# Rolling a matrix by 100 columns: how the last row groups of the long copy are cut

## The chip, the cores and the metric

The kernel runs on one core of a Trainium2 chip. The metric is the device time of a run in microseconds; for the kernel before it is the median of three runs, 816.32 us (815.55 to 818.43). Beside the runs there is one profiled execution, with its own span and trace; all durations of instructions and transfers come from it.

## The reference

```python
def setup_inputs():
    return {"x": np.random.randn(8192, 8192).astype(np.float32), "shift": 100}

def reference(x, shift):
    return np.roll(x, shift, axis=1)
```

Every row of the output is the row of the input turned to the right by 100 elements: `out[r, 100:]` is `x[r, :8092]`, and `out[r, :100]` is `x[r, 8092:]`. Nothing is computed; 268.4 MB are read and 268.4 MB are written.

## The kernel before, in words

With `s = 100`, the output's columns are split at `a = 256` (the next multiple of 128 above `s`, and 128 more). The two sides take different ways.

**The long side, columns 256 to 8191** (7,936 floats, 31,744 bytes a row), is copied straight from HBM to HBM, without a tile in between, by DMAs issued from SP (`nc.sync`) and ACT (`nc.scalar`). The rows are viewed as 128 blocks `c` of 64 rows; a block holds four groups `j`, and group `j` takes the rows `64c + 4e + j` for `e` from 0 to 15, so a group has 16 rows, four apart. The views `xm` and `om` (L36 to L37 of the code below) say this. The loop runs over blocks and groups in order (L41 to L43); even groups go to SP, odd ones to ACT, so each engine has its own queue with 256 of the 512 groups. A group is one DMA of 16 rows, 496 KB; in the last four blocks, which are 16 groups, it is two DMAs of 16 half rows (3,968 floats each, split at `mid = 4224`), 248 KB each. That makes 248 whole and 16 half pieces on each queue.

The order on each queue is the program's order. The framework gives the long side's DMAs eight semaphores, four to SP and four to ACT, taken in turn (108, 111, 113, 115 on SP and 107, 110, 112, 114 on ACT); an issue waits until the DMA that used its semaphore before has landed. A DMA raises its semaphore once for each of 16 DMA engines, each of which moves one of the 16 rows. SP waits at the end for all semaphores before the program closes.

**The short side, columns 0 to 255**, is done by GpSimd (POOL) and VectorE (DVE). For each of 16 strips of 512 rows, GpSimd loads the head of the rows in three DMAs (L72, L73, L76) into SBUF tiles, VectorE copies parts of one tile into another (L74, L77), and at the end GpSimd stores 16 tiles of 512 KB (L80). It uses a queue of its own. In the profiled execution its last store lands at 505.9 us.

The few lines that decide the pieces:

```python
mid = (a + n_cols) // 256 * 128
for c in range(blocks):
    parts = ((a, mid), (mid, n_cols)) if c >= blocks - 4 and a < mid else ((a, n_cols),)
    for j in range(4):
        for lo, hi in parts:
            engines[j % 2].dma_start(out=om[c, j, :, lo:hi], in_=xm[c, j, :, lo - s:hi - s])
```

Of the kernel before, what the change touches and what calls it, by code (L numbers as in the profile page):

```python
# [1 line left out]

# [4 lines left out]


@with_exitstack
def kernel(  # L10
    ctx: ExitStack,
    tc: tile.TileContext,
    x: bass.AP,
    shift: int,
    out: bass.AP,
):
    nc = tc.nc
    n_rows, n_cols = x.shape
    s = shift % n_cols
    a = -(-s // 128) * 128  # L20
    if 0 < a <= 384 and a + 128 <= n_cols:
        a += 128
    g = a - s
    P = nc.NUM_PARTITIONS
    engines = [nc.sync, nc.scalar]
    n_chunks = 16
    rows = n_rows // n_chunks

    xm = x.rearrange("(c e j) w -> c j e w", e=16, j=4)
    om = out.rearrange("(c e j) w -> c j e w", e=16, j=4)
    if a < n_cols:  # L36
        blocks = n_rows // 64  # L37
        mid = (a + n_cols) // 256 * 128
        for c in range(blocks):
            parts = ((a, mid), (mid, n_cols)) if c >= blocks - 4 and a < mid else ((a, n_cols),)  # L40
            for j in range(4):  # L41
                for lo, hi in parts:
                    engines[j % 2].dma_start(out=om[c, j, :, lo:hi], in_=xm[c, j, :, lo - s:hi - s])  # L43
    if a == 0:
        return


    if a > 512:
        for i in range(n_chunks):
            r = slice(i * rows, (i + 1) * rows)  # L50
            nc.gpsimd.dma_start(out=out[r, :s], in_=x[r, n_cols - s:])
            if g > 0:
                nc.gpsimd.dma_start(out=out[r, s:a], in_=x[r, :g])
        return

    Q = 4  # L60
    n_st = n_rows // (P * Q)
    reads = ctx.enter_context(tc.tile_pool(name="reads", bufs=n_st))
    heads = ctx.enter_context(tc.tile_pool(name="heads", bufs=n_st))
    xt = x.rearrange("(k p q) c -> k p q c", q=Q, p=P)
    ot = out.rearrange("(k p q) c -> k p q c", q=Q, p=P)
    tiles = []
    for k in range(n_st):
        t = reads.tile([P, Q - 1, a], x.dtype)
        h = heads.tile([P, Q, a], x.dtype)
        lead = bass.AP(tensor=x.tensor, offset=(k * P * Q + 1) * n_cols - s,  # L70
                       ap=[[Q * n_cols, P], [n_cols, Q - 1], [1, a]])
        nc.gpsimd.dma_start(out=t[:], in_=lead, single_packet=True)  # L72
        nc.gpsimd.dma_start(out=h[:, Q - 1, :s], in_=xt[k, :, Q - 1, n_cols - s:], single_packet=True)  # L73
        nc.vector.tensor_copy(h[:, :Q - 1, :s], t[:, :, :s])  # L74
        if g > 0:
            nc.gpsimd.dma_start(out=h[:, 0, s:], in_=xt[k, :, 0, :g], single_packet=True)  # L76
            nc.vector.tensor_copy(h[:, 1:, s:], t[:, :, s:])  # L77
        tiles.append(h)
    for k, h in enumerate(tiles):
        nc.gpsimd.dma_start(out=ot[k, :, :, :a], in_=h[:], single_packet=True)  # L80


# [1 line left out]
_INS = ['x', 'shift']  # L84
_OUTS = [((8192, 8192), 'float32')]

_NUMBERS = {'shift': 100}


# [26 lines left out]
```

## Time and profile before

| what | value |
|---|---|
| runs, median (lowest to highest) | 816.32 us (815.55 to 818.43) |
| profiled execution, span from first to last instruction | 813.9 us |
| last landing of the long side in it | 812.95 us |
| DMA packets and bytes of the span | 22,277 packets, 276.9 MB |
| mean rate of the DMA engines | 340 GB/s |
| SP's and ACT's issues of whole pieces | 248 each, 12.5 us from issue to landing (median) |
| SP's and ACT's issues of half pieces | 16 each, 5.9 us from issue to landing (median) |
| VectorE busy | 12.0 us |
| GpSimd busy | 41.1 us |

The median of the runs stands 2.4 us above the span of the profiled execution; the page has no time for what lies around the span. The bytes are counted once for each packet, though the long side reads and writes HBM. A "GB/s" of a stretch counts the packets that start in it. A "landing" is the event at which a DMA engine raises the semaphore of the DMA; a DMA of the long side has 16 of them, and "from issue to landing" is up to the last.

### The profile page before, as it was taken

What the parts mean: (1) busy time and instruction counts of PE and PEld (TensorE: products, weight loads), DVE (VectorE), ACT (ScalarE), POOL (GpSimd) and SP (SyncE); (2) the same over time, 40 slices, a digit from 0 to 9 for tenths busy, and PEclk for the clock granted to TensorE, in tenths of its full rate; (3) what the DMA queues carried; (4) which work ended last, traced back from release to release, by engine and by line L of the source; (5) the groups of instructions that cost most, each with busy time, mean ns of one, the idle gap of its engine ahead of it and who ended that gap; (6) DMA issues with size and microseconds to landing.
All of it is one profiled execution on the core that took longest, in us unless ns stands there. A gap on an engine that the chain in (4) does not pass through costs nothing. (4 is left out here: it accounts for less than half of the span.)

```text
span 813.9 us, 689 instructions
## 1 busy us (share of the span) xinstructions
DVE 12.0 (1%) x32; POOL 41.1 (5%) x68
## 2 busy tenths in 40 slices
DVE  0000000000000000000000000000000000000000
POOL 2000011111000100000000000000000000000000
DMA  9999999999999999999999999999999999999998
GB/s 314 346 340 344 353 346 350 344 351 344 346 355 346 345 362 354 353 357 354 355 355 349 342 335 331 335 332 325 335 328 332 334 337 334 332 337 332 334 314 293
DMA packets 22277, 276.90 MB, mean 340 GB/s; under 512 B 9472, under 2 KB 9728, under 8 KB 13824
## 3 DMA queue, kind: packets, MB, share of 16 engines
q1 hardware_dynamic: 8448, 130.04, 45.9%
q10 hardware_dynamic: 8448, 130.04, 44.3%
q0 software_dynamic: 5376, 16.78, 8.9%
q14 instruction: 5, 0.04, 0.0%
HBM read 268.44 MB, written 268.44 MB: 660 GB/s over the span
## 5 line engine op out<-in xcount | busy, mean ns | idle before, releaser
L80 POOL DMA_DIRECT2D out_dram<-h x16 | 11.4, 713 | 139.5 <-DMA out_dram<-h 92.5
L76 POOL DMA_DIRECT2D h<-in_x_dram x16 | 8.6, 540 | 158.4 <-DMA t<-in_x_dram 158.4
L72 POOL DMA_DIRECT2D t<-in_x_dram x16 | 12.2, 760 | 32.1 <-DMA h<-in_x_dram 31.3
L73 POOL DMA_DIRECT2D h<-in_x_dram x16 | 8.9, 558 | 32.7 <-DMA h<-in_x_dram 32.7
L74 DVE COPY h<-t 128x300 f32<-128x300 f32 x16 | 5.9, 367 | 268.4 <-DMA t<-in_x_dram 268.4
L77 DVE COPY h<-t 128x468 f32<-128x468 f32 x16 | 7.5, 468 | 0.0
L97 POOL MEMSET const-float32-0.0<- 128x1 f32 x1 | 0.1, 98 | 0.2 <-issue 0.2
L97 POOL MEMSET const-bfloat16-1.0<- 128x1 bf16 x1 | 0.1, 101 | 0.0
L97 POOL MEMSET const-float32-1.0<- 128x1 f32 x1 | 0.1, 98 | 0.0
L97 POOL MEMSET const-uint8-127<- 128x1 uint8 x1 | 0.1, 98 | 0.0
## 6 DMA issues: line engine op xcount, KB each, us to landing
out_dram<-in_x_dram ACTq DMA_DIRECT2D x248, 496.0 KB, 12.5
out_dram<-in_x_dram SPq DMA_DIRECT2D x248, 496.0 KB, 12.5
out_dram<-h POOLq DMA_DIRECT2D x16, 512.0 KB, 102.9
t<-in_x_dram POOLq DMA_DIRECT2D x16, 384.0 KB, 48.9
out_dram<-in_x_dram SPq DMA_DIRECT2D x16, 248.0 KB, 5.9
out_dram<-in_x_dram ACTq DMA_DIRECT2D x16, 248.0 KB, 5.9
h<-in_x_dram POOLq DMA_DIRECT2D x16, 78.0 KB, 41.9
h<-in_x_dram POOLq DMA_DIRECT2D x16, 50.0 KB, 47.2
```

What stands on the lines that cost most here:

```text
L72: nc.gpsimd.dma_start(out=t[:], in_=lead, single_packet=True)
L73: nc.gpsimd.dma_start(out=h[:, Q - 1, :s], in_=xt[k, :, Q - 1, n_cols - s:], single_packet=True)
L74: nc.vector.tensor_copy(h[:, :Q - 1, :s], t[:, :, :s])
L76: nc.gpsimd.dma_start(out=h[:, 0, s:], in_=xt[k, :, 0, :g], single_packet=True)
L77: nc.vector.tensor_copy(h[:, 1:, s:], t[:, :, s:])
L80: nc.gpsimd.dma_start(out=ot[k, :, :, :a], in_=h[:], single_packet=True)
L97: nc = _bacc.Bacc("TRN2", target_bir_lowering=False, num_devices=1)
```

## The change

Only the loop that issues the long side changes. The number of pieces of a group now depends on `left`, the number of groups from this one to the last: quarters for the last four groups, halves for the six before them, whole for all others.

```diff
         blocks = n_rows // 64
-        mid = (a + n_cols) // 256 * 128
+        def cuts(parts):
+            w = (n_cols - a) // parts // 128 * 128
+            return [(a + i * w, a + (i + 1) * w if i + 1 < parts else n_cols) for i in range(parts)]
+
         for c in range(blocks):
-            parts = ((a, mid), (mid, n_cols)) if c >= blocks - 4 and a < mid else ((a, n_cols),)
             for j in range(4):
-                for lo, hi in parts:
+                left = 4 * (blocks - c) - j
+                for lo, hi in cuts(4 if left <= 4 else 2 if left <= 10 else 1) if n_cols - a >= 512 else [(a, n_cols)]:
                     engines[j % 2].dma_start(out=om[c, j, :, lo:hi], in_=xm[c, j, :, lo - s:hi - s])
```

Halves are cut where they were (3,968 floats each). A quarter is 1,920 floats (7,680 bytes a row), the last of four 2,176 (8,704 bytes a row). Each queue then issues 251 whole pieces, 6 halves and 8 quarters, 265 in all, where it issued 248 and 16, 264 in all. The last block is all quarters, the block before it all halves, and of the block before that groups 2 and 3 are halves.

## The prediction

> **What bounds the kernel now.** I read the page first: its engine rows, its row of DMA shares and its queues. No engine computes on the path (VectorE 1% of the span, GpSimd 5%), the 16 DMA engines are at nine tenths or more in 39 of 40 slices, and the two hardware queues, SP's and ACT's, carry 260 of 277 MB:
>
> ```profile
> q1 hardware_dynamic: 8448, 130.04, 45.9%
> q10 hardware_dynamic: 8448, 130.04, 44.3%
> q0 software_dynamic: 5376, 16.78, 8.9%
> ```
>
> The columns are packets, MB and the share of the 16 engines' span. 8448 packets for 264 DMAs of a queue are 32 each: 16 of data, one row for each engine, and 16 that raise the semaphore. The third queue, GpSimd's column strip, has its last landing at 505.9 us (semaphore events of the trace), so nothing of it is left in the stretch that the change touches. The page's chain of waits ends on GpSimd and does not follow SP to the end; I don't use it. The view of the waits, for SP's queue, does:
>
> ```profile
> SPq L43 <- DMA out_dram<-in_x_dram: 667.0, 260, 4.5
> SPq L111 <- DMA out_dram<-in_x_dram: 5.4, 4, 2.4
> ```
>
> Of its 264 issues 260 wait for an earlier transfer, 667.0 us in all: only the first four don't. The issues' semaphores say which: each queue has four, taken in turn, so issue i waits until issue i-4 of its queue has landed on all 16 engines. **Eight pieces are in flight, whatever their size**: 8 x 508 KB of wholes, 8 x 254 KB of halves (a piece is 16 rows of 31,744 or 15,872 bytes). The second line is the drain behind SP's last issue. The source view of the copy line, over 700 to 781 us (wholes) and over 781 to 814 us (halves), gives the time from issue to landing:
>
> ```profile
> L43 SPq DMA_DIRECT2D out_dram<-in_x_dram x27: 509/509/510, 700.0 to 778.6; - x27
> ...
> DMA to landing us min/median/max: 11.2/12.2/12.8
> ```
> ```profile
> L43 SPq DMA_DIRECT2D out_dram<-in_x_dram x16: 509/510/510, 781.6 to 806.7; - x16
> ...
> DMA to landing us min/median/max: 4.7/5.9/9.4
> ```
>
> 12.2 us for 8 x 508 KB is 333 GB/s, 5.9 us for 8 x 254 KB is 344 GB/s: at either size what is in flight is just worked off in one round trip. Now the stretches, with DMA share and GB/s last:
>
> ```profile
> 700.00:781.00 81.00, 0.00 (x0) 0.00 (x0) 1.00 0.99 334
> 781.00:796.00 15.00, 0.00 (x0) 0.00 (x0) 1.00 0.88 301
> 796.00:811.00 15.00, 0.00 (x0) 0.00 (x0) 1.00 0.98 343
> 811.00:812.50 1.50, 0.00 (x0) 0.00 (x0) 1.00 0.11 42
> ```
>
> Wholes run at 334 GB/s; the step to halves at 781.6 us dips to 301; halves once settled are as fast as wholes. A row counts a packet where it starts, so data under way at a border must be put back: half of 16 x 31.7 KB = 0.25 MB at 781, half of 16 x 15.9 KB = 0.13 MB at 796. The step: 15 x 301 KB + 0.25 - 0.13 = 4.64 MB, 13.9 us' worth at 334 in 15.0 us, **1.1 us lost**. From 796 to the last packet's end (812.4 us): 15 x 343 + 1.5 x 42 KB + 0.13 MB = 5.34 MB, 16.0 us' worth in 16.4, **0.4 us lost**. All that a better end could win is about 1.5 us of 816, or 0.2%.
>
> **The change part by part.** The whole-row pieces grow from 248 to 251 on each queue, the halves fall from 16 to 6, and 8 quarters come last (6 of 7,680 bytes a row, 2 of 8,704). Bytes, rows, order of rows, GpSimd's work and the start are the same, so all is equal until the first half, which now goes out six groups later: 6 x 508 KB at 334 GB/s = 9.1 us after 781.6, at about 790.7 us. The data left from there are 16 - 6 = 10 groups in place of 16.
>
> (1) One more issue on each queue, 265 for 264. An issue takes 0.51 us and SP's median wait is longer; at 334 GB/s two queues need a quarter of 127 KB (the mean) every 2 x 127 / 334 = 0.76 us each, more than 0.51. Cost 0; if four issues become ready together they follow each other at 0.51 us, which 0.76 mostly covers. Upper bound one issue, 0.5 us.
>
> (2) The step from wholes to halves is moved, not removed: the same eight wholes are in flight before it. It costs the 1.1 us again. The cause is read from the landings: the first of a whole's 16 landings comes 6 us before its last (median spread 6.0 us in 700 to 781), so the fast engines have half of a 12.2 us window left, and when refills halve they run dry. In before the share stays low until 795, in after the first quarter goes out after six halves of a queue, where before had reached 792.2 us, so part of this dip runs into the next step. Change 0; bounds -0.4 (the last third left out) and 0.
>
> (3) A second step, from halves to quarters, is new. The trace has no such step; the nearest row is the first step, 1.1 us, at twice the sizes: spread of landings 2.1 us for halves (median) against 6.0, window 5.9 against 12.2. In proportion to the size it costs half: **+0.5 us**, bounds 0 (the smaller spread is covered) and +1.1 (as the first).
>
> (4) The quarters themselves. Eight hold 1.02 MB, 3.0 us of work at 334 GB/s. Their round trip has no row either. Its parts: 1.4 us from the first issue (0.74 us) to the first packet (2.14 us), 0.5 us from the last packet's end (812.43) to the last landing (812.95), and two packets' times, its own and the other queue's: a half's packet is 0.72 us in the mean (least 0.59), so 2 x 0.36. That is 2.6 us on an engine with nothing queued. On top comes the lag of the slowest engine, 2.1 us for halves; in proportion 1.0. Sum 3.6 to 4.7 us against 3.0 us of data in flight: the queue is starved. The same sum for halves, 1.9 + 1.4 + 2.1 = 5.4 us, is under their 6.1 us of data and close to the 5.9 seen, which is why halves kept the rate. Sixteen quarters are two rounds of eight; the first still has halves in front of it and is (3). The second loses 3.6 - 3.0 = **+0.6 us**; bounds 0 and 4.7 - 3.0 = +1.7. I take the lag in proportion, because it went 6.0 to 2.1 from wholes to halves.
>
> The Trainium skill, "DMA: Bandwidth & Descriptors", section on the anatomy of one DMA, fits a software-queue DMA as about 2.0 us fixed plus its bytes at 436 GB/s. By that a quarter is an estimated 2.3 us, below 3.0, nothing is starved and term (4) is 0. The rows above speak against it: the quickest half in this trace took 4.7 us, where the page's fit would give 2.6.
>
> (5) The end. When the last piece is taken up, engines finish unevenly by about one packet. The 0.4 us lost after 796 shrinks with the piece: **-0.4 us** if all goes, 0 if it was not of the end at all.
>
> Sum: 0 + 0 + 0.5 + 0.6 - 0.4 = +0.7 us. The profiled execution's span is 813.9 us, its last landing at 812.95; the runs' median, 816.32, lies 2.4 us above that span, and I carry this over unchanged: 814.6 us of span, **817.0 us** for the median.
>
> **The rivals.** A measurement of this kernel can tell about 0.3% (2.4 us) from no change; the three runs shown span 2.9 us.
>
> *No starvation.* Terms (3) and (4) at 0, the end better by 0.4, the dip cut short by 0.4: 816.32 - 0.8 = 815.5 us. For it: halves ran at 343 GB/s, so a smaller piece costs nothing by itself. Against it: the round trip's 1.9 us of fixed parts do not shrink. Within 0.3% too.
>
> *A shorter end that shows.* Every loss after 781 comes back, 1.5 us: 814.8 us. That still is only 0.2%; to be over 0.3% faster the runs must fall low as well, which the spread of the runs allows (the lowest of before is 0.8 under its median). Chance 0.15.
>
> *Starved quarters, the other sign.* In-order waits on four semaphores a queue make one slow engine hold up all eight slots; if a quarter's lag stays at the halves' 2.1 us or grows (single half packets took up to 2.0 us), both rounds are starved. The price is two rounds of (round trip - 3.0) less 0.4; it is over 2.4 us from a round trip of 4.4 us on. With 4.7 us: 2 x 1.7 - 0.4 = +3.0, 819.3 us. For it: packets' stalls come singly and need not shrink with the size. Against it: the last round drains, and the spread fell by more than half when the size halved. Chance 0.23.
>
> *The change does not do what it says.* The order of the issues on the two queues shows 251 wholes, 6 halves and 8 quarters on each, and the splits start at multiples of 512 bytes in the output; nothing to wait for is added but the four semaphores. No chance of its own.
>
> **How the numbers follow.** Within 0.3% (forecast and no starvation together) 0.62, faster 0.15, slower 0.23. The range goes from 1.5 us won with 0.4 for the runs' own scatter (814.4) to the starved case (819.3).
>
> **What would show it.** In the changed profile: stretches equal to before up to about 790; a dip to about 0.85 share behind the first half at 790.7; issue to landing of the quarters at 3.6 us, not 3.0 (covered) or 4.7 (starved); a GB/s of 260 to 290 in the last 6 us of data; the last landing at 813 to 814.5 us. I am wrong if the changed kernel's stretch before 780 us differs, since nothing there is changed, or if the settled halves no longer keep the rate of wholes.

## The result, and the profile after

| | runs | median (lowest to highest), us |
|---|---|---|
| before | 10 | 817.09 (815.45 to 818.43) |
| after | 10 | 819.44 (817.19 to 820.91) |

The ratio on record is 1.0023, with a 95% interval from 1.0013 to 1.0032: 1.9 us slower (1.1 to 2.6). The two medians of the table stand 2.35 us apart; the ratio is what is used below. On the scale of the forecast's 816.32 us that is 818.2 us, where 817.0 was forecast. The sign came out, and by the bound of 0.3% it is no change that one measurement could tell; ten runs a side can, and the forecast of +0.7 us lies below their interval.

(In the kernel before, the views stand at L34 and L35 and the loop at L39 to L43, not at L36 to L37 and L41 to L43 as said above. The copy line is L43 there and L46 in the changed kernel.)

The profiled execution has a span of 818.3 us (its run: 820.1 us). The runs from here on list a time about 1.8 us above their span; by that, before's profiled execution, with its 813.9 us, took about 815.7 us, 1.4 us under the median of ten. The page's queue rows (packets, MB, share):

```profile
q1 hardware_dynamic: 8480, 130.04, 46.3%
q10 hardware_dynamic: 8480, 130.04, 44.1%
q0 software_dynamic: 5376, 16.78, 8.2%
```

32 packets more on each queue are the one DMA more; the bytes are equal. SP's waits:

```profile
SPq L46 <- DMA out_dram<-in_x_dram: 673.0, 260, 5.3
SPq L114 <- DMA out_dram<-in_x_dram: 3.2, 1, 3.2
```

The drain behind SP's last issue fell from 5.4 to 3.2 us, as eight quarters in place of eight halves are left then. Read alone, that looks like a gain. The stretches (DMA share and GB/s last) show that it was paid for before:

```profile
700.00:781.00 81.00, 0.00 (x0) 0.00 (x0) 1.00 1.00 333
...
794.00:805.00 11.00, 0.00 (x0) 0.00 (x0) 1.00 0.87 292
805.00:815.00 10.00, 0.00 (x0) 0.00 (x0) 1.00 0.82 281
815.00:816.60 1.60, 0.00 (x0) 0.00 (x0) 1.00 0.52 167
```

The first half goes out at 794.0 us, the first quarter at 805.2. After the step to halves (0.87, as before's 0.88) the engines never fill up again: the quarters follow at a share of 0.82, where before had run at 0.98 and 343 GB/s from 796 to 811. The source view of the copy line from 805.1 us on holds the quarters alone:

```profile
L46 SPq DMA_DIRECT2D out_dram<-in_x_dram x8: 509/510/527, 805.2 to 813.3; - x8
...
DMA to landing us min/median/max: 3.0/3.8/5.1
```

3.8 us for 1.02 MB in flight is 267 GB/s.

The two profiled executions differ by 4.4 us, but not all of that is the change's. I worked out, from the packets' starts, durations and sizes, how long each execution took from the moment that N MB were left (packets under way counted in part) to its last packet's end, and took off N MB at 334 GB/s. That "loss" is compared below, since it leaves out the first 750 us, in which both kernels do the same and single executions scatter: with 20 MB left the changed kernel's execution was already 2.6 us late (753.7 us against 751.0).

| us lost against 334 GB/s in the last | 20 MB | 10 MB | 3 MB | 0.5 MB |
|---|---|---|---|---|
| before | 1.5 | 1.6 | 0.8 | 1.0 |
| after | 3.1 | 3.0 | 2.0 | 0.9 |

1.6 us of the tail are lost more, 1.2 of them in the last 3 MB, where the quarters are. These are single executions: a second one of the changed kernel (e5_after) lost 2.7 us in the last 20 MB, not 3.1.

### The profile page after: what moved, and what is told of

The parts are those of the page before. It is cut to its first block, busy times and chain, and to the rows that moved or that the text cites. A ratio compares the mean times of both kernels' runs of the same rounds, so it can differ in the third digit from the quotient of the medians.

```text
span 818.3 us, 691 instructions
## 1 busy us (share of the span) xinstructions
DVE 12.0 (1%) x32; POOL 41.3 (5%) x68
## 4 chain that ended last, share of the span: by engine, by line
DMA 32%; another core or an unknown queue 16%; POOL 1%; issue 1%; POOLq 0%; PEldq 0%
DMA h<-in_x_dram 28%; DMA t<-in_x_dram 4%; POOL out_dram L83 1%; POOL h L76 0%; POOL t L75 0%; POOLq L114 0%; POOL h L79 0%; POOLq L83 0%; PEldq L114 0%
```

## The experiments

My theory is **starvation**: eight DMAs are in flight whatever their size; the round trip, from a DMA's issue to its last landing, has parts that do not shrink with the piece; eight quarters hold less work than a round trip lasts. The rivals: the **step** (any change of size costs once), the **packet** (short packets cost by themselves), and the **stretch** (the halves' stretch was cut from 16 groups to 6, so that the step lies nearer to the end). All kernels are the changed one with another rule for the pieces; only the loop is touched.

**Sixty-four groups in quarters (e1_q64): starvation made large.**

```diff
-                for lo, hi in cuts(4 if left <= 4 else 2 if left <= 10 else 1) if n_cols - a >= 512 else [(a, n_cols)]:
+                for lo, hi in cuts(4 if left <= 64 else 1) if n_cols - a >= 512 else [(a, n_cols)]:
```

> Quarters for the last 64 groups (256 quarters), no halves. Starvation theory (eight quarters in flight, 1.02 MB, against a round trip of 3.6 to 4.0 us as in the changed kernel's profile): 32.5 MB move at 254 to 282 GB/s in place of 334, so 115 to 128 us for 97 us, 18 to 31 us slower than before, and the stretch shows that rate throughout. Step theory (only the change of size costs, once): about 2 us slower, as the change itself. Packet theory (each shorter packet costs a little by itself; an undisturbed 7,680-byte packet takes 291 ns, half of 592 is 296): no more than 2 us slower.

Measured 847.21 us, ratio 1.0356 (1.0340 to 1.0372): 29 us slower. Here are the stretch and the source view of the copy line in the middle of the quarters:

```profile
740.00:830.00 90.00, 0.00 (x0) 0.00 (x0) 1.00 0.80 255
```
```profile
L46 SPq DMA_DIRECT2D out_dram<-in_x_dram x91: 509/510/716, 739.5 to 829.8; - x91
...
DMA to landing us min/median/max: 3.1/4.0/4.6
```

One DMA in flight after another takes 4.0 us, eight of 127 KB give 8 x 127 / 4.0 = 254 GB/s, and 255 is what is seen over 90 us. That these two agree is bookkeeping: with eight always in flight they must, as they do for wholes. What says that the engines wait for work is the share of 0.80 where wholes have 0.99: a fifth of their time is idle, so neither the shorter packets nor the 16 semaphore packets of each DMA fill it. Nor is it the issuing: 91 issues of 0.51 us take 46 of SP's 90 us. 32.5 MB at 255 in place of 334 GB/s is 30 us more, and 29 were timed. The step theory (2 us) and the packet theory (2 us) fall.

**The same packets with more in flight (e2_m64).** One DMA carries the quarter of all four groups of a block, 64 rows; all groups ahead of these go whole. The lines that make the views `xb` and `ob` are left out here.

```diff
+            if c >= blocks - 16:
+                for i, (lo, hi) in enumerate(cuts(4)):
+                    engines[i % 2].dma_start(out=ob[c, :, :, lo:hi], in_=xb[c, :, :, lo - s:hi - s])
+                continue
```

> The same packets of 7,680 and 8,704 bytes for the last 64 groups, but one DMA takes a quarter of the columns of all four groups of a block: 64 rows, 4 packets for each engine, 508 KB in flight for each DMA, eight in flight. Starvation theory: as fast as whole pieces in that stretch, 334 GB/s and 12 us from issue to landing, within 1.5 us of before. Packet theory: the same loss as with 256 separate quarters. Step theory: no step in what is in flight, so as whole pieces.

Measured 819.95 us, ratio 1.0027 (1.0016 to 1.0038).

```profile
740.00:800.00 60.00, 0.00 (x0) 0.00 (x0) 1.00 0.99 329
```
```profile
L47 SPq DMA_DIRECT2D out_dram<-in_x_dram x20: 511/511/593, 742.7 to 799.6; - x20
...
DMA to landing us min/median/max: 9.0/12.2/15.0
```

Share 0.99 and 329 GB/s with the packet sizes that gave 255 GB/s above: short packets cost about 1.2% in this execution (329 against 333 from 600 to 700 us), and what is in flight decides. The 2.2 us over before are more than the 1.5 that I allowed, and they are not in the stretch alone: the last 0.5 MB took 3.0 us against before's 2.5. This kernel ends on DMAs of 508 KB, without halves, and the kernel with wholes to the end (e8_whole, below) is 1.0016 by that alone.

**Sixty-four groups in halves (e3_h64).** The same edit with `2 if left <= 64 else 1`.

> Halves for the last 64 groups, no quarters. Starvation theory: eight halves hold 6.1 us of work against a round trip of about 5.5, so 334 to 344 GB/s and within 1 us of before. Step theory: the same, one step as before. If halves too are a little starved: their stretch at 320 GB/s or less, 4 us or more slower.

Measured 817.24 us, ratio 0.9994 (0.9984 to 1.0004).

```profile
740.00:800.00 60.00, 0.00 (x0) 0.00 (x0) 1.00 1.00 330
```
```profile
L46 SPq DMA_DIRECT2D out_dram<-in_x_dram x39: 509/510/548, 740.4 to 798.6; - x39
...
DMA to landing us min/median/max: 5.1/6.1/7.7
```

With a share of 1.00, halves are not starved.

**Thirds (e10_t64), the size between.** `3 if left <= 64 else 1`.

> Thirds for the last 64 groups (10,240 and 11,264 bytes a row, 169 KB a DMA). Eight hold 1.35 MB, 4.05 us of work at 334 GB/s. Starvation theory with the parts of the prediction: 1.9 us fixed, two packets of 0.48 us, and a lag between the 1.4 us of quarters and the 2.1 us of halves: a round trip of 4.3 to 5.0 us, 270 to 315 GB/s, 6 to 23 us slower than before. If the fixed parts overlap better than that: 334 GB/s and no loss.

Measured 832.47 us, ratio 1.0185 (1.0160 to 1.0209), 15 us slower.

```profile
740.00:815.00 75.00, 0.00 (x0) 0.00 (x0) 1.00 0.87 293
```
```profile
L46 SPq DMA_DIRECT2D out_dram<-in_x_dram x83: 509/510/645, 725.5 to 819.5; - x83
...
DMA to landing us min/median/max: 3.6/4.6/5.4
```

8 x 169 KB in 4.6 us is 294 GB/s, and 293 is seen. The round trips are 4.0, 4.6 and 6.1 us for 127, 169 and 254 KB. A line through the first two starts at about 2 us and rises by about 0.015 us a KB (2.2 and 0.0143 from the medians as shown, 2.0 and 0.0155 from 3.99 and 4.64 us); it meets "eight pieces at 334 GB/s" at 0.23 to 0.24 MB a piece, an estimate from two points. By it halves, at 0.25 MB, lie just above the edge.

**Which part of the change costs.** Two kernels do one part alone: halves for the last ten groups and no quarters (e4_h10), and quarters for the last four with halves for the twelve before them, so that the step stays where it was (e6_h12q4). The changed kernel ran once more beside the second (e5_after). The two added lines below are the one of e4_h10 and the one of e6_h12q4.

```diff
-                for lo, hi in cuts(4 if left <= 4 else 2 if left <= 10 else 1) if n_cols - a >= 512 else [(a, n_cols)]:
+                for lo, hi in cuts(2 if left <= 10 else 1) if n_cols - a >= 512 else [(a, n_cols)]:
+                for lo, hi in cuts(4 if left <= 4 else 2 if left <= 16 else 1) if n_cols - a >= 512 else [(a, n_cols)]:
```

> The change without its quarters: the last 10 groups in halves, the others whole. Starvation theory: the loss of 1.6 us (last 20 MB of the profile) goes, within 0.5 us of before, and the last 10 MB take 31 to 32 us as before. If the shorter stretch of halves were the cause: still about 2 us slower than before.

> Halves for twelve groups, quarters for the last four: before with only its last four groups cut finer, so the step to halves stays where it was. Starvation theory (the loss is that of the quarters): 1.3 to 1.9 us slower than before, the last 3 MB at 260 to 290 GB/s. Stretch theory (the loss comes from a step to halves that lies too near the end): within 0.5 us of before.

> The changed kernel once more, beside the three that follow. Starvation and stretch theories alike: 1.0013 to 1.0032 of before, as the first time.

| | ratio to before | 95% interval | lost in last 3 MB | in last 0.5 MB |
|---|---|---|---|---|
| e4_h10, shorter halves alone | 1.0012 | 0.9999 to 1.0025 | 1.2 | 1.0 |
| e6_h12q4, quarters alone | 1.0024 | 1.0014 to 1.0034 | 1.8 | 0.7 |
| e5_after, both | 1.0025 | 1.0015 to 1.0036 | 1.6 | 0.9 |

The quarters alone cost as much as the whole change, so the stretch theory is not needed; whether the shorter halves cost anything is not settled, for e4_h10's interval just takes in 1. Its 1.0 us is more than the 0.5 expected, and its last 10 MB took 32.5 us, not 31 to 32. The traces speak against a dearer step: between 10 and 3 MB left, where the step to halves lies, the four executions with the step at sixteen groups (before, e6_h12q4, and e7_h14q2 and e9_h12p4 below) lost 1.2 us in the mean (0.8 to 1.5), the three with the step at ten (after, e4_h10, e5_after) 1.1 (0.9 to 1.3), and two without a step there (e3_h64, e8_whole) 0.2. In e6_h12q4 the source view from 804.5 us on, quarters alone, shows the same round trip again:

```profile
L46 SPq DMA_DIRECT2D out_dram<-in_x_dram x8: 509/510/510, 804.5 to 812.0; - x8
...
DMA to landing us min/median/max: 3.4/3.9/4.6
```

**The cure at full size (e9_h12p4).** Twelve groups in halves and the last block in quarters' packets, but two groups to a DMA, so that eight hold 2 MB again. The lines that make the views `xm2` and `om2` are left out here, and the rule for the other groups is `2 if left <= 16 else 1`.

```diff
+            if c == blocks - 1:
+                for j in (0, 2):
+                    for i, (lo, hi) in enumerate(cuts(4)):
+                        engines[i % 2].dma_start(out=om2[c, :, j:j + 2, lo:hi], in_=xm2[c, :, j:j + 2, lo - s:hi - s])
+                continue
```

> Halves for twelve groups as in the kernel before, and the last block in the quarters' packets (7,680 and 8,704 bytes), but each DMA carries a quarter of two groups: 32 rows, two packets for each engine, 245 to 279 KB, so that eight in flight hold as much as eight halves. Starvation theory: the 1.9 us of e6_h12q4 go, within 0.7 us of before, the last 3 MB lose 0.8 us against 334 GB/s as with halves, issue to landing stays near 6 us. Packet theory: 1.3 to 1.9 us slower, as with single quarters.

Measured 817.15 us, ratio 0.9999 (0.9985 to 1.0013); 0.7 us lost in the last 3 MB.

```profile
L48 SPq DMA_DIRECT2D out_dram<-in_x_dram x4: 571/582/621, 807.0 to 811.4; - x4
...
DMA to landing us min/median/max: 5.9/6.0/7.1
```

The quarters' packets are at the end, without the quarters' loss: the loss was that of the bytes in flight.

**Fewer quarters (e7_h14q2).** `4 if left <= 2 else 2 if left <= 16 else 1`: eight quarters, one round.

> Halves for 14 groups, quarters for the last two: eight quarters, which go out while halves are still in the rings, so no round of quarters waits for quarters. Starvation theory: between before and 0.7 us slower, the second round's loss is gone and the step's half microsecond stays. If any quarter costs: 1 us or more slower. If a finer end pays: 0.4 us faster.

Measured 817.90 us, ratio 1.0008 (0.9996 to 1.0020), 0.8 us lost in the last 3 MB, as in before. With the second round gone the loss is gone to within the measurement; a finer end that pays 0.4 us does not show (the interval reaches from 0.3 us faster to 1.6 slower).

**No cut at all (e8_whole).** Every group is whole, `cuts(1)`.

> All 512 groups whole. No step and nothing starved, but the slowest of the 16 engines ends up to 6 us (the spread of a whole's landings) behind the first, where halves have 2 us. If that lag counts at the end: 1.5 to 3 us slower than before, with the last 2 MB taking 8 us or more in place of 6.9. If the engines' lag does not matter: 1 us faster, since the step's loss is saved.

Measured 819.24 us, ratio 1.0016 (1.0003 to 1.0029). The last 1 MB took 6.0 us, 3.0 more than at 334 GB/s; before took 4.0.

```profile
800.00:810.00 10.00, 0.00 (x0) 0.00 (x0) 1.00 0.99 330
810.00:815.00 5.00, 0.00 (x0) 0.00 (x0) 1.00 0.39 152
```

The engines are full until 810 us, then the share is 0.39: as if six of the sixteen still had work. So there are two ways to lose at the end, and halves stand between them. The 1.3 us (0.2 to 2.4) lie just below the 1.5 to 3 expected.

**Halves throughout (e11_h512),** `cuts(2)` for every group, tried as a version without any step.

> All 512 groups in halves. Starvation theory: eight halves still cover the round trip, so the rate holds, no step near the end; within 1 us of before, at best 1 us faster. If GpSimd's strips, which share the engines in the first 506 us, lengthen the round trip beyond 6.1 us of the two queues' own data: several us slower, all of it in that part.

Measured 820.20 us, ratio 1.0047 (1.0028 to 1.0066). Its tail is as good as that of e3_h64 (0.5 us lost in the last 3 MB), so the loss is not there. The stretches say where something changed:

```profile
0.00:100.00 100.00, 12.05 (x32) 36.22 (x61) 1.00 0.99 368
100.00:200.00 100.00, 0.00 (x0) 5.01 (x7) 1.00 0.99 358
200.00:300.00 100.00, 0.00 (x0) 0.00 (x0) 1.00 1.00 333
```

GpSimd's strips, whose last store landed at 505.9 us in before, are done at 159.0 us (VectorE's 32 copies are all in the first 100). In the twelve other profiled executions, all with wholes in that part, this store lands between 473 and 531 us, so shorter pieces on the hardware queues let the third queue go ahead. Some 2.4 us are lost by 600 us: 71.7 MB of the long side are left then, against 70.4 to 71.3 (mean 70.9) in those twelve. Why the whole is some 4 us longer was not tried.

No version was measurably faster than the kernel before; the nearest, e3_h64, is at 0.9994 with 1 inside its interval.

## Why the prediction was right in its sign and too small

*What bounds it.* Eight pieces in flight held in every run; engines full but for the end held wherever the pieces were halves or wholes, and settled halves kept the rate (330 GB/s in e3_h64). The sum of all that the end could win was put at 1.5 us, and nothing tried won that much.

*(1) One more issue, 0.* Nothing contradicts it: issues still take 0.51 us, and the quarters' issues of a queue stand about 1.2 us apart (805.2 to 813.3 us for eight), so the queue waits for landings and not for issuing.

*(2) The step is moved, 0.* Held: a share of 0.87 behind the first half (0.88 in before), and the loss between 10 and 3 MB is equal for both places of the step. It came at 794.0 us, not 790.7; that execution was 2.6 us late at 753 us already. The prediction named a stretch before 780 us that differs as a sign of being wrong. The rate there is the same (333 and 334 GB/s from 700 to 781), and I read the lateness as scatter in a part that is equal in both kernels: seven executions with that part unchanged (after, e4_h10 to e9_h12p4) reach 20 MB left between 752.4 and 754.5 us, and before's, a quick one by its span, is the earliest of all, 751.0.

*(3) and (4), step and starved quarters, +0.5 and +0.6.* The mechanism of (4) is shown: by the engines' share in e1_q64 and e10_t64, and by its cure in e2_m64 and e9_h12p4. The round trip was forecast as 3.6 to 4.7 us with 3.6 taken; it is 3.8 to 4.0. The lag of the slowest engine, put at 1.0 us in it, is 1.3 to 1.5 (median time from first to last landing of a quarter in after, e5_after, e6_h12q4). The size of both terms together is near: in the last 3 MB the executions with four quartered groups lost 2.0, 1.6 and 1.8 us (after, e5_after, e6_h12q4), those with halves to the end 0.8, 1.2 and 0.5 (before, e4_h10, e3_h64), a difference of means of 0.95 us for the 1.1 forecast. The split is not shown. e7_h14q2 has the step to quarters and no second round, and its execution lost 0.8 us there, as before's did; by that the step costs nothing and the second round all. Its time (+0.7 us, -0.3 to 1.6) leaves room for the 0.5. That the sum came out so near may be luck.

The Trainium skill's fit ("DMA: Bandwidth & Descriptors", on the anatomy of one DMA: about 2.0 us fixed, plus bytes at 436 GB/s) had put this term at 0. That fit is for a DMA of the software queue; these go by the hardware queues. Its fixed part is near the 2 us at which the line through quarters and thirds starts. Its slope is not found again: here a KB costs about 0.015 us, as 65 to 70 GB/s would. My reading, not tested apart, is that eight DMAs share the engines and that the slowest of 16 engines ends each. The measurement decides: 4.0 us, not 2.3.

*(5) The end, -0.4.* **This step failed.** "The 0.4 us lost after 796 shrinks with the piece": the last 0.5 MB cost 0.9, 0.9 and 0.7 us with quarters and 1.0, 1.0, 0.4 with halves (the same six executions): no gain in the mean, though the halves alone scatter by more than the 0.4 us at stake. The last quarters are themselves a round in which engines stand idle (a share of 0.52 from 815.0 to 816.6 us of after), and e7_h14q2, where the last round is quarters without a second, ends no better (0.9). In place of the 0.4 us the runs show a gain of nothing, 0.8 us against 0.8 in the mean, as far as six executions can tell. Without this term the sum is +1.1 us, at the lower edge of the measured 1.1 to 2.6. The right sign hung on the other two terms being larger than this one.

*What stays open.* From +1.1 to the 1.9 us timed (2.0 in the second measurement, 1.2 to 2.9) some 0.8 us have no place that I can show, if they are there at all: the interval reaches down to the 1.1. The profiled executions lost 1.0 us more than before's in the last 3 MB and about 1.4 in the last 10 (3.0, 2.5 and 3.3 against 1.6), but there is only one execution of before with a trace, and e4_h10's (2.6) lies more than two thirds of the way. A part may be the shorter stretch of halves, which 1.0012 (0.9999 to 1.0025) neither shows nor excludes; e6_h12q4, without it, is as slow as the change, which speaks against it.

*The rivals.* "No starvation" (815.5 us) fell with e1_q64. "Starved quarters" on the other side asked for a round trip above 4.4 us; it was 3.8 to 4.0, and so stayed short of 0.3%. That the last landing came at 816.98 us, outside the 813 to 814.5 forecast and 4.0 us after before's, is 1.6 us of tail and 2.6 us from ahead of it. The last 6 us of data (810.6 to 816.6 us) ran at 238 GB/s, below the 260 to 290 forecast.

## What to carry to other kernels

Where an engine may have only so many DMAs in flight, the size of a piece sets how much work waits in the queues; multiply count by bytes, divide by the rate, and compare with an estimate of what the smaller piece would take from issue to landing, before cutting finer (here 3.0 us of work against 3.6 estimated and 3.8 to 4.0 measured). The time that the present pieces take does not tell it: while the engines are full, it equals the time that the work in flight takes. A shorter drain behind the last issue is no gain if the pieces before it run at 255 GB/s in place of 334, as quarters did in e1_q64. To have short packets at the end without that, put more rows into each DMA, and keep the number of bytes in flight.

## What the runs showed that I had not expected

By the estimate above the kernel sat beside the edge: halves of 254 KB ran at 330 GB/s and a full share, thirds of 169 KB at 293, quarters of 127 KB at 255, all with eight in flight. And wholes, with the most in flight, end badly: at the end of e8_whole the engines lay so far apart that the last 1 MB took 6.0 us, against 3.3 in e3_h64. The more is in flight, the further the engines drift apart: 6 us between the first and last landing of a whole and 2 us of a half (medians in before). The size of the packets is not what does it, for e2_m64's 508 KB DMAs of quarter packets spread by 6 us too, and e9_h12p4's of 245 to 279 KB by 2.
